# A hybrid decoder layer on one core: squares of the first norm off GpSimd, a third score buffer, value projections of N=512, and decode retention in steps

## The chip, the cores and the metric

The kernel runs on one core of a Trainium2 chip. The metric is the device time of one execution in microseconds. All inputs start in HBM and all outputs end there. Engines are called PE (TensorE; its weight loads PEld), DVE (VectorE), ACT (ScalarE), POOL (GpSimd) and SP (SyncE, here a queue that issues transfers).

## What is computed

One layer of a decoder that mixes retention and sliding-window attention, on 1024 prompt tokens and 64 decode tokens (8 sequences of 8), with a model width of 1024. The core of the reference:

```python
hn = rms_norm(x, norm_mix_gain)
q_r, k_r, v_r, g_r, q_s, k_s, v_s = jnp.split(hn @ w_in, cuts, axis=-1)   # 4 x 512, 512, 128, 128
o_r, new_ret = retention(q_r, k_r, v_r, ret_state, chunk)                 # 8 heads of 64, chunks of 128
o_r = rms_norm(o_r) * jax.nn.silu(g_r)
q_s, k_s = rms_norm(q_s, q_norm_gain), rms_norm(k_s, k_norm_gain)
o_s = swa_prompt(...) or swa_sample(...)     # window 128, 8 query heads on 2 kv heads, sinks, ALiBi
h = x + jnp.concatenate([o_r, o_s], axis=-1) @ w_out
hf = rms_norm(h, norm_ffn_gain)
return h + jnp.square(jax.nn.relu(hf @ w_up)) @ w_down, new_ret, new_k, new_v
```

One retention step on a chunk, per head:

```python
scores = einsum('ld,md->lm', q, k) * intra
o = scores @ v + (q * q_decay) @ s
s = s * s_decay + (k * k_decay).T @ v
```

The prompt starts from a zero state and has 8 chunks; each decode sequence starts from a state of its own.

## The kernel before, in words

**Numbers.** Most products are made in fp32 accuracy from three matmuls: each operand is split into a high part (rounded, made on ACT) and a low part (the rest, made on DVE or POOL), and `mm3` (L178 to L180) adds hi x hi, lo x hi and hi x lo into one PSUM tile. In the trace, L178, L179 and L180 are these three, whatever the product. Small products in retention are plain fp32 matmuls, each of which the trace shows as two.

**Tokens.** The 1088 tokens lie in chunks of 384, 384 and 320 columns and in token tiles t = 0 to 7 of 128; tile t = 8 is the decode tile, whose last 64 rows count.

**Stages.** PE's work in the trace runs in this order.
- Front (0 to 43 us): x and the first weights are loaded; `split_scaled` makes hnh (ACT, L136) and hnl (DVE, L137) of the normed input, without the row factor, which is applied to results later. `square_sum` adds the squares for that factor into rsb: chunks 0 and 1 on POOL (L144, L146), chunk 2 on ACT and DVE (L152, L153). PE runs the attention queries (psq); their squares (sqq) are read from PSUM by ACT. `inv_rms` sums over partitions and makes the factor rst (psrm).
- Key and value projection of the attention and the rest of the queries (to 120 us).
- Attention (to some 275 us): 8 blocks of 128 queries by 2 kv heads are 16 units. Each has scores (scp, L400; scaled and masked by DVE at L402 into a tile of tag "s"), a softmax (ACT, DVE, and POOL's last multiply at L366), transposes (ppp, L371) and the product with v (po, L422). Between them PE runs the retention's query, key and gate projections (psf, psg).
- Decode attention (s8, transposes pps, product po): the result is split into mhs and mls, which are stored in `ms_hi_d` and `ms_lo_d` in DRAM.
- Value projections: `value_block(t)` makes two groups of 24 matmuls 128x256 (pst), each read by one ACT instruction into half of vtr (L581). `retention_block(8)`, the decode retention, has scores rsr8, transposed keys pkr8, the product with v ror8, the product with the state pcr8 (added to ror8 through oc), and the state update pur8. Then come prompt retention blocks t = 0 to 4, each with one value tile ahead of it: scores rsr, transposed keys pkr, outputs ror, state update pur, and transposes pm of the mixed result. Their split operands lie in one tile of slot 8 (qkb), from which the store of the decode state has to be read first.
- When the value weights are dead, `proj.close()` frees their space; mixah, mixal (L781) and the raw output weights (L789) are loaded there, and the first output projection (pso) runs among retention blocks 5 to 7.
- From 420 us on, the rest of the output projection, and the MLP in Strassen-like products (psx, psy, psz, psd).

**What sets the order.** Instructions of each engine are put in order by a scheduler that simulates the program; tiles in pools are reused, and a reused tile waits for what last read it. SP issues transfers in its own order, so that a waiting one holds back those behind it.

Of the kernel before, what the change touches and what calls it, by code (L numbers as in the profile page):

```python
# [36 lines left out]
def hymba_layer(ctx: ExitStack, tc: tile.TileContext, a: dict, o: dict):  # L37
# [101 lines left out]
    def square_sum(acc, src, k, nm, pool=False):  # L139

        cw = src.shape[-1]
        if pool:
            sq = acc if k == 0 else sp.tile([P, 384], F32, tag="qkst", name=f"sq{nm}_{k}")[:, :cw]
            nc.gpsimd.tensor_tensor(sq, src, src, ALU.mult)  # L144
            if k:
                nc.gpsimd.tensor_tensor(acc, acc, sq, ALU.add)  # L146
            return
        if k == 0:
            nc.scalar.activation(acc, src, AF.Square)
        else:  # L150
# [2 lines left out]
            nc.vector.tensor_tensor(acc, acc, sq[:, :cw], ALU.add)  # L153
# [142 lines left out]
    for k in range(8):  # L296
        square_sum(rsb[:, 768:1088], xs[2][:, k, :], k, "m2")
# [81 lines left out]
    def swa_block(c):  # L379
# [5 lines left out]
        for kv in range(2):  # L385
# [8 lines left out]
            st = sp.tile([P, 4, 256], F32, tag="s", name="s" + nm)  # L394
# [70 lines left out]
    s8 = sp.tile([P, 4, 256], F32, tag="s", name="s8")[:, :, :192]  # L465
# [81 lines left out]
    w_v = [wload(a["w_in"][9 + i], 8, f"wv{i}") for i in range(2)]  # L547
# [26 lines left out]

    vts = {}

    def value_block(t):
        vt = vts[t] = rp.tile([P, 512], F32, tag="vt", name=f"vtr{t}", bufs=5)
        for i in range(2):
            ps = proj_tok(t, w_v[i], psA.tile([P, 512], F32, tag="mm", name="pst"))  # L580
            nc.scalar.activation(vt[:, i * 256 : i * 256 + 256], ps[:, :256], AF.Copy, scale=rst[:, t : t + 1])  # L581

    def retention_block(t):
        nonlocal state
        off, _, _ = tok_tile(t)
        nm = f"r{t}"
        vt = vts[t]
        qt, kt, gt = loaded8 if t == 8 else ret_load(t)

        pts = []  # L590
        if t == 8:
            for hh in range(2):
                ps = psB.tile([P, 512], F32, tag="t1", name="rs" + nm)
                p0 = hh * 64
                for p_ in range(4):
                    nc.tensor.matmul(
                        ps[64:128, p_ * 64 : p_ * 64 + 64], kt[p0 : p0 + 64, p_, 64:128], qt[p0 : p0 + 64, p_, 64:128],
                        start=True, stop=True,
                    )
                pt = rp.tile([P, 4, 128], F32, tag="rpt", name="rpt" + nm, bufs=3)  # L600
                nc.vector.tensor_tensor(
                    pt[64:128, :, 64:128], ps[64:128, :256].rearrange("p (h l) -> p h l", h=4),
                    intraS[64:128, hh::2, 64:128], ALU.mult,
                )
                pts += [pt[:, p_, :] for p_ in range(4)]
            pts = [pts[(h % 2) * 4 + h // 2] for h in range(8)]
        else:

            nc.scalar.copy(kh, kt)
            nc.gpsimd.tensor_tensor(kl, kt, kh.bitcast(F32), ALU.subtract)  # L610
            for hh in range(2):
                q_ = slice(hh * 64, hh * 64 + 64)
                nc.scalar.copy(qbh[q_, :, hh, :], qt[q_])
                nc.vector.tensor_tensor(qbl[q_, :, hh, :], qt[q_], qbh[q_, :, hh, :].bitcast(F32), ALU.subtract)
            for i in range(2):
                ps = psB.tile([P, 512], F32, tag="t1", name="rs" + nm)
                for p_ in (2 * i, 2 * i + 1):
                    cc = (p_ % 2) * 256
                    mm3(ps[:, cc : cc + 256], kh[:, p_, :], kl[:, p_, :], qbh[:, p_, :, :], qbl[:, p_, :, :], True, True)
                pt = rp.tile([P, 4, 128], F32, tag="rpt", name="rpt" + nm, bufs=3)  # L620
                nc.vector.tensor_tensor(
                    pt, ps.rearrange("p (h l) -> p h l", h=4), intra[:, 4 * i : 4 * i + 4, :], ALU.mult
                )
                pts += [pt[:, h, :] for h in range(4)]

        pk = psB.tile([P, 512], F32, tag="t2", name="pk" + nm)
        for p_ in range(4):
            nc.tensor.transpose(pk[:, p_ * 128 : p_ * 128 + 128], kt[:, p_, :], ident)
        kd = rp.tile([P, 512], F32, tag="kd", name="kd" + nm, bufs=1)
        nc.vector.tensor_tensor(  # L630
            kd.rearrange("p (h d) -> p h d", h=8), pk.rearrange("p (h d) -> p h d", h=8),
            (kdec8 if t == 8 else kdec).unsqueeze(2).broadcast_to([P, 8, 64]), ALU.mult,
        )

        cross = 0 < t < 8
        rr = slice(64, 128) if t == 8 else slice(0, 128)
        nr = 64 if t == 8 else 128
        po = psB.tile([P, 512], F32, tag="t3", bufs=1, name="ro" + nm)
        for h in range(8):
            for q_ in (slice(64, 128),) if t == 8 else (slice(0, 64), slice(64, 128)):  # L640
                nc.tensor.matmul(
                    po[q_, h * 64 : h * 64 + 64], pts[h][rr, q_], vt[rr, h * 64 : h * 64 + 64],
                    start=h == 0, stop=h == 7 and t == 0,
                )
        if t == 8:

            for hh in range(2):
                r_ = slice(hh * 64, hh * 64 + 64)
# [4 lines left out]
            pc = psB.tile([P, 512], F32, tag="t2", name="pc" + nm)
            pcv = pc.rearrange("p (q h b n) -> p q h b n", q=4, h=2, b=4)
            for p_ in range(4):
                for bp in range(4):
                    nc.tensor.matmul(
                        pcv[:, p_, :, bp, :], s0[:, p_, 2 * bp : 2 * bp + 2, :].rearrange("p b e -> p (b e)"),
# [658 lines left out]
```

## Time and profile before

| what | value |
|---|---|
| median of 3 runs | 1229.61 us (1229.16 to 1233.59) |
| profiled execution | 1229.86 us |
| its span on the core | 1228.1 us |
| busy: PE, DVE, POOL, ACT | 97%, 70%, 45%, 41% |
| chain that ended last | PE 79%, DVE 10%, DMA 4%, POOL 3% |
| mean granted PE clock | 0.986 |

The span is what the profiler saw on the engines; the profiled execution's own time has 1.8 us more around it. A row of a table by stretch has the stretch, its length, then busy time and instruction count of PE, PEld, DVE, ACT and POOL, the granted clock as a share of full speed, the busy share of the DMA engines, and GB/s. A row of the timeline has start, duration, engine, line, operation, output and inputs, shapes, how many instructions it joins, and in brackets how long the engine had been idle and for what. Matmuls are pipelined: what counts is the time from one start to the next.

### The profile page before, as it was taken

The numbers are of one execution on the slowest core, as the hardware profiler recorded it, in microseconds if no ns is written. First come the engines' busy times: TensorE is split into PE (matmuls) and PEld (weight loads), VectorE is DVE, ScalarE is ACT, GpSimd is POOL, SyncE is SP. The second block draws the span as 40 slices with busy tenths as digits, with TensorE's granted clock in tenths as the row PEclk, the third lists the DMA queues.
The fourth block names the chain that finished last, engine by engine and source line by source line (L and its number), as shares of the span: only waits on it lengthen the run. The fifth ranks groups of instructions, "written<-read, shape, count | busy, mean of one in ns | idle before, by whom it ended". The sixth has DMA issues, their size and how long they took to land.

```text
span 1228.1 us, 23929 instructions
## 1 busy us (share of the span) xinstructions
PE 1192.1 (97%) x9621; PEld 1151.4 (94%) x9621; DVE 855.1 (70%) x1508; ACT 502.2 (41%) x1032; POOL 558.1 (45%) x463
## 2 busy tenths in 40 slices
PE   7999999998998999989999999999999999999998
PEld 6999989897977899889999999999989999999998
DVE  7856776734036878788767666666578779888776
ACT  6343444572023434454444444444463333333231
POOL 8425333332225546467666666666672232253000
PEclk9999999999799999899999999999989999999999
DMA  6211234332316644433434444444584455543215
GB/s 238 71 60 60 95 99 161 100 111 72 107 53 205 211 137 132 145 104 121 167 130 146 144 143 152 143 152 160 173 299 146 142 179 166 188 166 127 74 56 182
DMA packets 102277, 169.46 MB, mean 138 GB/s; under 512 B 11999, under 2 KB 68255, under 8 KB 101911
## 3 DMA queue, kind: packets, MB, share of 16 engines
q1 hardware_dynamic: 88279, 123.24, 30.1%
q10 hardware_dynamic: 11328, 35.79, 8.9%
q0 software_dynamic: 2560, 8.91, 2.3%
q8 instruction: 75, 1.23, 0.4%
q14 instruction: 35, 0.29, 0.1%
HBM read 114.30 MB, written 53.61 MB: 137 GB/s over the span
## 4 chain that ended last, share of the span: by engine, by line
PE 79%; DVE 10%; DMA 4%; POOL 3%; issue 2%; ACT 2%; SPq 0%; ACTq 0%; DVEq 0%; POOLq 0%
PE psd L179 8%; PE psd L180 8%; PE psd L178 8%; PE psx L178 5%; PE psx L180 5%; PE psx L179 5%; PE psf L179 2%; PE psf L180 2%; PE psf L178 2%; PE psz L178 2%; PE psz L180 2%; PE psz L179 2%; PE pst L178 2%; PE pst L179 2%; PE pst L180 2%
## 5 line engine op out<-in xcount | busy, mean ns | idle before, releaser
L178 PE MATMUL psd<-uh,wd_w 128*128 128x272 f32 x896 | 259.4, 290 | 2.2 <-ACT a L1183 2.2
L179 PE MATMUL psd<-uh,wd_w 128*128 128x272 f32 x896 | 260.7, 291 | 0.6 <-DVE wd_w L758 0.6
L180 PE MATMUL psd<-ul,wd_w 128*128 128x272 f32 x896 | 259.1, 290 | 0.8 <-DVE ul L758 0.8
L178 PEld LDWEIGHTS psd<-uh,wd_w 128*128 128x128 f32 x896 | 170.4, 190 | 2.4 <-ACT a L1183 2.4
L180 PEld LDWEIGHTS psd<-ul,wd_w 128*128 128x128 f32 x896 | 169.8, 190 | 1.0 <-DVE ul L758 1.0
L179 PEld LDWEIGHTS psd<-uh,wd_w 128*128 128x128 f32 x896 | 169.7, 189 | 1.1 <-DVE wd_w L758 1.1
L1187 DVE TENSOR_TENSOR a<-a,psd 128x272 f32<-128x272 f32 x248 | 101.1, 429 | 40.8 <-PE psd L180 40.8
L758 DVE TENSOR_TENSOR wu_w<-wu_s,wu_w 128x512 fp32r<-128x512 f32 x64 | 59.5, 929 | 50.3 <-ACT wu_w L757 49.3
L757 ACT CAST wd_w<-wd_s 128x512 fp32r<-128x512 f32 x64 | 37.3, 619 | 116.8 <-PE psd L180 101.0
L758 DVE TENSOR_TENSOR ul<-ur,uh 128x1088 fp32r<-128x1088 f32 x56 | 83.1, 1510 | 2.1 <-ACT uh L757 2.1
L179 PE MATMUL psx<-op_0h,wu_w 128*128 128x272 f32 x256 | 74.2, 290 | 2.0 <-DVE wu_w L758 2.0
L178 PE MATMUL psx<-op_0h,wu_w 128*128 128x272 f32 x256 | 74.8, 292 | 0.7 <-ACT m L1066 0.5
L178 PE MATMUL psx<-op_1h,wu_w 128*128 128x272 f32 x256 | 74.7, 292 | 0.5 <-ACT m L1066 0.5
L1052 DVE SCALAR_TENSOR_TENSOR m<-m,rsf 128x272 f32<-128x272 f32 x96 | 73.2, 762 | 2.7
L180 PE MATMUL psx<-op_1l,wu_w 128*128 128x272 f32 x256 | 74.5, 291 | 0.0
L180 PE MATMUL psx<-op_0l,wu_w 128*128 128x272 f32 x256 | 74.4, 291 | 0.0
L179 PE MATMUL psx<-op_1h,wu_w 128*128 128x272 f32 x256 | 74.2, 290 | 0.0
L366 POOL TENSOR_TENSOR sp<-sp,ssp 128x1024 f32<-128x1024 f32 (+1 forms) x16 | 28.6, 1787 | 94.7 <-DVE ssp L365 69.5
L1094 POOL TENSOR_TENSOR r4t<-r3t,r4t 128x272 f32<-128x272 f32 x64 | 64.0, 1011 | 1.2
L757 ACT CAST uh<-ur 128x1088 fp32r<-128x1088 f32 x56 | 59.6, 1099 | 11.4 <-PE psd L179 9.1
L178 PE MATMUL psf<-hnh,wqk_hi 128*128 128x384 f32 (+1 forms) x192 | 63.2, 329 | 0.0
L180 PE MATMUL psf<-hnl,wqk_hi 128*128 128x384 f32 (+1 forms) x192 | 63.0, 328 | 0.0
(329 smaller groups left out, 3798.3 us busy)
## 6 DMA issues: line engine op xcount, KB each, us to landing
ur<-u_d SPq DMA_DIRECT2D x52, 544.0 KB, 5.0
u_d<-r4t SPq DMA_DIRECT2D x32, 544.0 KB, 3.9
wu_r<-in_w_up ACTq DMA_DIRECT2D x32, 512.0 KB, 4.3
wd_r<-in_w_down ACTq DMA_DIRECT2D x30, 512.0 KB, 6.9
u_d<-r3t SPq DMA_DIRECT2D x32, 408.0 KB, 3.1
y<-in_xY POOLq DMA_DIRECT2D x16, 272.0 KB, 3.2
y_d<-y POOLq DMA_DIRECT2D x16, 272.0 KB, 3.4
yt<-y_d SPq DMA_DIRECT2D x16, 272.0 KB, 3.9
```

The costliest lines, as they stand in the source:

```text
L178: nc.tensor.matmul(ps, lh, rh, start=first, stop=False, skip_group_check=more)
L179: nc.tensor.matmul(ps, ll, rh, start=False, stop=False, skip_group_check=more)
L180: return nc.tensor.matmul(ps, lh, rl, start=False, stop=last, skip_group_check=more)
L366: nc.gpsimd.tensor_tensor(s, s, ss.unsqueeze(2).broadcast_to([P, 4, n]), ALU.mult)
L757: nc.scalar.copy(hi, src)
L758: lo_eng.tensor_tensor(lo, src, hi.bitcast(F32), ALU.subtract)
L1052: nc.vector.scalar_tensor_tensor(t_, src, 0.0, rsf[:, s, h, :], ALU.max, ALU.mult)
L1094: sub = lambda o_, p_, q_: nc.gpsimd.tensor_tensor(o_, p_, q_, ALU.subtract)
L1187: nc.vector.tensor_tensor(to, to, ps, ALU.add)
```

## The change

It has five parts.
1. All squares of the first norm are made on ACT and added on DVE (`squares_of`): 16 squares and 14 adds of 128x384 leave POOL. The adds of one chunk are written behind the splits of the next.
2. The tag "s" of the attention has three buffers, where it had two.
3. The value weights are laid out in two halves of k with 512 columns each, so a token tile takes 24 matmuls 128x512 and one eviction 128x512.
4. The decode retention is a generator of seven steps, which `queued` starts behind the last matmul of a value tile, and whose last matmul the next value tile follows. From t = 1 on, value tile t + 3 is queued behind retention block t, not ahead of it.
5. Tiles are placed under others that are dead by then: dummy tiles fix the order of the pool rp and of a new pool rv (for v, mixed results, decayed queries, loaded queries and keys). The split operands of retention 0 to 4 lie in three weight tiles ("raw"), and those of 5 to 7 in slot 8.

```diff
-    def square_sum(acc, src, k, nm, pool=False):
+    def square_sum(acc, src, k, nm):
         cw = src.shape[-1]
-        if pool:
-            sq = acc if k == 0 else sp.tile([P, 384], F32, tag="qkst", name=f"sq{nm}_{k}")[:, :cw]
-            nc.gpsimd.tensor_tensor(sq, src, src, ALU.mult)
-            if k:
-                nc.gpsimd.tensor_tensor(acc, acc, sq, ALU.add)
-            return
...
     for c, (c0, cw) in enumerate(CH):
...
         hn.append((hi, lo))
+        if c:
+            squares_of(c - 1)
...
-            st = sp.tile([P, 4, 256], F32, tag="s", name="s" + nm)
+            st = sp.tile([P, 4, 256], F32, tag="s", name="s" + nm, bufs=3)
...
-    w_v = [wload(a["w_in"][9 + i], 8, f"wv{i}") for i in range(2)]
+    w_v = [wload(a["w_in"][9 + i], 4, f"wv{i}") for i in range(2)]
...
     def value_block(t):
-        vt = vts[t] = rp.tile([P, 512], F32, tag="vt", name=f"vtr{t}", bufs=5)
-        for i in range(2):
-            ps = proj_tok(t, w_v[i], psA.tile([P, 512], F32, tag="mm", name="pst"))
-            nc.scalar.activation(vt[:, i * 256 : i * 256 + 256], ps[:, :256], AF.Copy, scale=rst[:, t : t + 1])
+        vt = vts[t] = rv.tile([P, 512], F32, tag="vt", name=f"vtr{t}", bufs=5)
+        _, c, r = tok_tile(t)
+        ps = psA.tile([P, 512], F32, tag="mm", name="pst")
+        for k in range(8):
+            lh, ll = (x[:, k, r : r + 128] for x in hn[c])
+            ins = mm3(ps, lh, ll, w_v[k // 4][0][:, k % 4, :], w_v[k // 4][1][:, k % 4, :], k == 0, k == 7)
+        nc.scalar.activation(vt, ps, AF.Copy, scale=rst[:, t : t + 1])
+        return ins.ins
...
-    for t in (8, 0, 1, 2):
-        value_block(t)
-    mt8 = retention_block(8)
...
+    def queued(ins, f, *args):
+        with tc.issue_after(ins):
+            return f(*args)
+
+    decode = retention_decode()
+    value_block(8)
+    ins = value_block(0)
+    ins = queued(ins, next, decode)
+    ins = queued(ins, value_block, 1)
+    ins = queued(ins, next, decode)
+    ins = queued(ins, value_block, 2)
+    ins = queued(ins, next, decode)
...
+    qbh, qbl, kh, kl = split_space([ring.tile([P, 1024], F32R, tag="raw", name=f"qk{i}", bufs=3) for i in range(3)])
...
     for t in range(5):
-        if t < 5:
-            value_block(t + 3)
+        if t == 0:
+            for _ in range(2):
+                ins = queued(ins, next, decode)
+            ins = queued(ins, value_block, 3)
+            for _ in range(2):
+                ins = queued(ins, next, decode)
         held[t] = retention_block(t)
+        if t:
+            ins = queued(ins, value_block, t + 3)
```

Three places show how the order changes. First, DVE in the front. In both, hnl are the low parts of the normed input (L137), wq_lo and wkv_lo those of weights, rq and qs results of the queries; before:

```order
L137 SCALAR_TENSOR_TENSOR hnl_167<-x_75,c_g_mix,hnh_166 128x384 x2
L79 TENSOR_TENSOR wq_lo<-wq_raw_90,wq_hi 128x512
L137 SCALAR_TENSOR_TENSOR hnl_167<-x_75,c_g_mix,hnh_166 128x384 x2
L137 SCALAR_TENSOR_TENSOR hnl_185<-x_76,c_g_mix,hnh_184 128x384 x5
L289 COPY rq<-prq 128x6
L137 SCALAR_TENSOR_TENSOR hnl_185<-x_76,c_g_mix,hnh_184 128x384
L289 COPY rq<-prq 128x6
L137 SCALAR_TENSOR_TENSOR hnl_185<-x_76,c_g_mix,hnh_184 128x384 x2
L137 SCALAR_TENSOR_TENSOR hnl_203<-x_77,c_g_mix,hnh_202 128x320 x2
L113 TENSOR_SCALAR qg_115<-c_qkg 128x1
L111 TENSOR_SCALAR nsinks<-c_sinks 128x9
```

and after, where the adds of the squares are L147:

```order
L147 TENSOR_TENSOR rsb<-rsb,sqm_6_218 128x384
L137 SCALAR_TENSOR_TENSOR hnl_185<-x_76,c_g_mix,hnh_184 128x384 x2
L147 TENSOR_TENSOR rsb<-rsb,sqm_7_221 128x384
L137 SCALAR_TENSOR_TENSOR hnl_185<-x_76,c_g_mix,hnh_184 128x384 x2
L147 TENSOR_TENSOR rsb<-rsb,sqm_1_243 128x384
L137 SCALAR_TENSOR_TENSOR hnl_185<-x_76,c_g_mix,hnh_184 128x384
L147 TENSOR_TENSOR rsb<-rsb,sqm_2_246 128x384
L137 SCALAR_TENSOR_TENSOR hnl_185<-x_76,c_g_mix,hnh_184 128x384 x2
L113 TENSOR_SCALAR qg_115<-c_qkg 128x1
L111 TENSOR_SCALAR nsinks<-c_sinks 128x9
L137 SCALAR_TENSOR_TENSOR hnl_185<-x_76,c_g_mix,hnh_184 128x384
L147 TENSOR_TENSOR rsb<-rsb,sqm_3_249 128x384
```

The adds stand among the splits; of the 14 adds of chunks 0 and 1, ten stand ahead of the splits of chunk 2 (hnl_225, which begin right behind the last row), one among these and three behind them. The results of the queries (rq, qs), which stood among the splits of chunks 1 and 2, now come behind all of them.

Second, PE at the decode attention: pps are its transposes, po its product, pst the first value tiles, psg gate projections. Before, 72 value matmuls have gone ahead, and the two steps stand back to back:

```order
L179 MATMUL pst<-wv_hi,hnl_203 128x256
L180 MATMUL pst<-wv_lo,hnh_202 128x256
L371 MATMUL pps<-c_ident,s_2171 128x128 [waits PE_49,Pool_49]
L371 MATMUL pps<-c_ident,s_2171 128x128 [waits Activation_49] x3
L371 MATMUL pps<-c_ident,s_2171 64x128 [waits PE_49]
L371 MATMUL pps<-c_ident,s_2171 64x128 x3
L495 MATMUL po_2239<-pt_2237,v_285 64x256 [waits DVE_49]
L495 MATMUL po_2239<-pt_2237,v_285 64x256
L498 MATMUL po_2239<-pt_2230,smp 64x32 [waits DMAHW7_49]
L498 MATMUL po_2239<-pt_2230,smp 64x32 x15
L178 MATMUL pst<-wv_hi,hnh_166 128x256 [waits Activation_49]
L179 MATMUL pst<-wv_hi,hnl_167 128x256
```

After, 19 gate matmuls follow the transposes; the last three of these, and what stands behind them:

```order
L172 MATMUL psg<-hnh_224,wg_hi 128x320
L173 MATMUL psg<-hnh_224,wg_lo 128x320
L174 MATMUL psg<-hnl_225,wg_hi 128x320
L172 MATMUL pst<-wv_hi,hnh_224 128x512 [waits DVE_49]
L173 MATMUL pst<-wv_hi,hnl_225 128x512
L174 MATMUL pst<-wv_lo,hnh_224 128x512
L172 MATMUL pst<-wv_hi,hnh_224 128x512
L173 MATMUL pst<-wv_hi,hnl_225 128x512
L174 MATMUL pst<-wv_lo,hnh_224 128x512
L172 MATMUL pst<-wv_hi,hnh_224 128x512
L492 MATMUL po_2239<-pt_2237,v_285 64x256 [waits DVE_49]
L492 MATMUL po_2239<-pt_2237,v_285 64x256
```

So 19 gate and seven value matmuls stand between the transposes and the product. On ACT, the evictions of the value tiles that follow, before:

```order
L505 CAST mhs<-po_2239 128x8x4x8 [waits DMAHW6_49,PE_49]
L581 ACTIVATE vtr_3393<-pst,rst 128x256 [waits DMAHW5_49,DMAHW3_49,DVE_49]
L581 ACTIVATE vtr_3393<-pst,rst 128x256
L581 ACTIVATE vtr_3446<-pst,rst 128x256
L581 ACTIVATE vtr_3446<-pst,rst 128x256 [waits PE_49]
```

and after (qk are the split operands of retention 0, filled with zeros at L929):

```order
L502 CAST mhs<-po_2239 128x8x4x8 [waits DMAHW3_49,PE_49]
L592 ACTIVATE vtr_3413<-pst,rst 128x512 [waits PE_49,Pool_49]
L929 ACTIVATE qk_3587<-qdec 128x1024 [waits DMAHW2_49,Pool_49]
L929 ACTIVATE qk_3588<-qdec 128x1024 [waits Pool_49]
L592 ACTIVATE vtr_3440<-pst,rst 128x512 [waits PE_49]
```

The first eviction waited for two transfers and now waits for PE and POOL.

Third, PE behind the last value matmul, with the retention blocks' products by the names above; before, retention 2's outputs and retention 3's scores follow it:

```order
L179 MATMUL pst<-wv_hi,hnl_203 128x256
L180 MATMUL pst<-wv_lo,hnh_202 128x256
L641 MATMUL ror_4062<-vtr_3552,rptr_4044 64x64 [waits DVE_49]
L641 MATMUL ror_4062<-vtr_3552,rptr_4044 64x64 x7
L641 MATMUL ror_4062<-vtr_3552,rptr_4053 64x64 x8
L691 MATMUL ror_4062<-state_3381,qdr_4079 128x128 [waits Pool_49]
L691 MATMUL ror_4062<-state_3381,qdr_4079 128x128 x3
L737 MATMUL pm<-c_ident,mtr_3962 128x128 [waits PE_49]
L737 MATMUL pm<-c_ident,mtr_3962 128x128 x3
L179 MATMUL rsr_4183<-qkb 128x256 [waits Pool_49]
L180 MATMUL rsr_4183<-qkb 128x256
L178 MATMUL rsr_4183<-qkb 128x256
```

After, it is followed by retention 3's outputs and update and retention 5's scores:

```order
L173 MATMUL pst<-wv_hi,hnl_225 128x512
L174 MATMUL pst<-wv_lo,hnh_224 128x512
L721 MATMUL ror_3996<-vtr_3606,rptr_3978 64x64 [waits DVE_49,Activation_49]
L721 MATMUL ror_3996<-vtr_3606,rptr_3978 64x64 x7
L721 MATMUL ror_3996<-vtr_3606,rptr_3987 64x64 x8
L729 MATMUL ror_3996<-state_3386,qdr_4013 128x128 [waits Pool_49]
L729 MATMUL ror_3996<-state_3386,qdr_4013 128x128 x3
L736 MATMUL pur_4019<-vtr_3606,kdr_3994 64x64 [waits DVE_49]
L736 MATMUL pur_4019<-vtr_3606,kdr_3994 64x64 x7
L766 MATMUL pm<-c_ident,mtr_3916 128x128 [waits PE_49]
L766 MATMUL pm<-c_ident,mtr_3916 128x128 x3
L172 MATMUL rsr_4245<-qkb 128x256 [waits Activation_49]
```

Retention 2's outputs, and the scores of retention 3 and 4, stand ahead of the last value tile.

More of the change, by code (lines that the diff above doesn't have):

```diff
@@ L201, in hymba_layer, with squares_of @@
     rsb = nt.tile([P, T], F32, tag="rsb", name="rsb", bufs=1)
+    def squares_of(c):
+        c0, cw = CH[c]
+        for k in range(8):
+            square_sum(rsb[:, c0 : c0 + cw], xs[c][:, k, :], k, f"m{c}")
     for c, (c0, cw) in enumerate(CH):
@@ L295, in hymba_layer @@
     proj_q(0, w_q0)
-    for k in range(8):
-        square_sum(rsb[:, 768:1088], xs[2][:, k, :], k, "m2")
+    squares_of(2)
     sl8 = slot(8, F32R, "kk")
@@ L464, in hymba_layer @@
     nc.sync.dma_start(o["vc"][0:120], vc[8:128])
-    s8 = sp.tile([P, 4, 256], F32, tag="s", name="s8")[:, :, :192]
+    s8 = sp.tile([P, 4, 256], F32, tag="s", name="s8", bufs=3)[:, :, :192]
     for tt in range(2):
@@ L534, in hymba_layer @@
     rp = ret.enter_context(tc.tile_pool(name="ret", bufs=2, reuse_waits="tile"))
+    for tag, n in (("gt", 4), ("osq", 1), ("kd", 1)):
+        for i in range(n):
+            rp.tile([P, 512], F32, tag=tag, name=f"{tag}_", bufs=n)
     def ret_load(t):
@@ L537, in ret_load @@
         qt, kt = (
-            rp.tile([P, 4, 128], F32, tag=n + "8" * (t == 8), name=f"{n}{t}", bufs=1 + (t < 8)) for n in ("qt", "kt")
+            (rp if t == 8 else rv).tile([P, 4, 128], F32, tag=n + "8" * (t == 8), name=f"{n}{t}", bufs=1 + (t < 8))
+            for n in ("qt", "kt")
         )
@@ L573, in hymba_layer @@
     nc.vector.tensor_tensor(ident2, ident[:, 0:64], ident[:, 64:128], ALU.add)
+    for i in range(3):
+        rp.tile([P, 512], F32, tag="rpt", name="rpt_", bufs=3)
+    rv = ret.enter_context(tc.tile_pool(name="retv", bufs=2, reuse_waits="tile"))
+    for tag, n in (("vt", 5), ("mt", 2), ("qd", 1)):
+        for i in range(n):
+            rv.tile([P, 512], F32, tag=tag, name=f"{tag}_", bufs=n)
     vts = {}
     def value_block(t):
-        vt = vts[t] = rp.tile([P, 512], F32, tag="vt", name=f"vtr{t}", bufs=5)
@@ L579, in value_block @@
-        for i in range(2):
-            ps = proj_tok(t, w_v[i], psA.tile([P, 512], F32, tag="mm", name="pst"))
[L581 to L624, printed above, removed]
@@ new lines, in value_block, with scaled_keys @@
+        vt = vts[t] = rv.tile([P, 512], F32, tag="vt", name=f"vtr{t}", bufs=5)
+        _, c, r = tok_tile(t)
+        ps = psA.tile([P, 512], F32, tag="mm", name="pst")
+        for k in range(8):
+            lh, ll = (x[:, k, r : r + 128] for x in hn[c])
+            ins = mm3(ps, lh, ll, w_v[k // 4][0][:, k % 4, :], w_v[k // 4][1][:, k % 4, :], k == 0, k == 7)
+        nc.scalar.activation(vt, ps, AF.Copy, scale=rst[:, t : t + 1])
+        return ins.ins
+    def scaled_keys(kt, dec, nm, tag="kd"):
@@ L626, in retention_block @@
         pk = psB.tile([P, 512], F32, tag="t2", name="pk" + nm)
         for p_ in range(4):
[L628 to L629 removed]
+            ins = nc.tensor.transpose(pk[:, p_ * 128 : p_ * 128 + 128], kt[:, p_, :], ident)
+        kd = (rv if tag == "mt" else rp).tile([P, 512], F32, tag=tag, name="kd" + nm, bufs=1 + (tag == "mt"))
         nc.vector.tensor_tensor(
             kd.rearrange("p (h d) -> p h d", h=8), pk.rearrange("p (h d) -> p h d", h=8),
[L632 removed]
+            dec.unsqueeze(2).broadcast_to([P, 8, 64]), ALU.mult,
@@ L633, in retention_block @@
         )
[L635 to L644, printed above, removed]
@@ L719, in retention_block, with head_norm @@
+        return kd, ins
+    def head_norm(po, mt, rr, nm):
+        nr = rr.stop - rr.start
         sq = rp.tile([P, 512], F32, tag="osq", name="osq" + nm, bufs=1)
@@ L724, in retention_block @@
         nc.gpsimd.tensor_tensor(r[rr], r[rr], mhalf[rr].broadcast_to([nr, 8]), ALU.pow)
-        mt = mixtok8 if t == 8 else rp.tile([P, 512], F32, tag="mt", name="mt" + nm)
         nc.vector.tensor_tensor(
@@ L931, in hymba_layer @@
     mix_block(4, *held[4])
+    sl8c = slot(8, F32R, "qkb")
+    qbh, qbl, kh, kl = split_space([sl8c[:, i : i + 1024] for i in (0, 1024, 2048)])
     for t in (5, 6, 7):
```

233 lines of the change are left out of this document (149 added, 84 removed).

## Prediction

> **What bounds the kernel now.** I read the page's first part and its chain, then busy time by stretch, then PE's waits stretch by stretch, and last single lines.
>
> ```profile
> span 1228.1 us, 23929 instructions
> PE 1192.1 (97%) x9621; PEld 1151.4 (94%) x9621; DVE 855.1 (70%) x1508; ACT 502.2 (41%) x1032; POOL 558.1 (45%) x463
> ```
>
> PE (TensorE) is busy 97% of the span, so time can only come from three things: less matmul work, PE's waits, or stretches in which the granted clock is halved. The table by stretch (columns: length, busy time of PE, weight loads, DVE, ACT, POOL, then granted clock, DMA share, GB/s) says where these lie.
>
> ```profile
> 0.00:42.75 42.75, 35.31 (x252) 29.25 (x253) 35.71 (x41) 20.63 (x38) 34.31 (x45) 1.00 0.50 173
> 289.34:384.78 95.44, 89.52 (x753) 78.97 (x752) 33.44 (x59) 24.80 (x47) 32.12 (x27) 0.93 0.26 72
> 384.78:397.63 12.85, 9.76 (x135) 8.91 (x134) 9.07 (x25) 4.37 (x8) 6.15 (x6) 1.00 0.97 340
> 397.63:420.00 22.37, 19.71 (x200) 18.53 (x199) 17.38 (x34) 9.79 (x19) 11.97 (x11) 0.92 0.80 251
> 420.00:1228.10 808.10, 791.79 (x6364) 786.45 (x6363) 605.00 (x957) 326.93 (x648) 389.43 (x330) 0.99 0.45 149
> ```
>
> PE stands in the front (0 to 43 us), around the value projections (289 to 385) and around the first output projection (385 to 420). The change touches all three. From 420 us on it touches nothing but the last retention blocks, and I take that stretch as it is.
>
> **Squares off GpSimd.** In the front, PE waits for the low parts of the normed input (hnl, L137 on DVE).
>
> ```profile
>   DVE hnl L137: 13.2, 24
> L271 ACT ACTIVATE sqq<-psq x5: 437/490/493, 19.7 to 41.5; 128x384 f32<-128x384 f32 x4, 128x320 f32<-128x320 f32 x1
> L137 DVE SCALAR_TENSOR_TENSOR hnl<-x,c_g_mix,hnh 128x384 fp32r<-128x384 f32 x16 | 17.6, 1144 | 5.0 <-ACT hnh L136 5.0
> L137 DVE SCALAR_TENSOR_TENSOR hnl<-x,c_g_mix,hnh 128x320 fp32r<-128x320 f32 x8 | 9.2, 1200 | 0.0
> L79 DVE TENSOR_TENSOR wq_lo<-wq_raw,wq_hi 128x512 fp32r<-128x512 f32 x4 | 4.2, 1049 | 1.2 <-ACT wq_hi L77 1.2
> 5.09 0.62 DVE L137 SCALAR_TENSOR_TENSOR hnl<-x,c_g_mix,hnh 128x384 fp32r<-128x384 f32 x1 [4.15 <-ACT hnh L136]
> 5.70 0.69 DVE L79 TENSOR_TENSOR wq_lo<-wq_raw,wq_hi 128x512 fp32r<-128x512 f32 x1
> 49.13 0.48 DVE L153 TENSOR_TENSOR rsb<-rsb,sqm 128x320 f32<-128x320 f32 x1
> ```
>
> The first line is PE's and its weight loads' wait for hnl before the query projection (us, times). The same hnl instruction takes 0.62 us while GpSimd is idle (at 5.09) and 1.14 to 1.20 on average beside GpSimd's squares (34.31 us of GpSimd in this stretch); wq_lo takes 0.69 against 1.05. With GpSimd out of the way the 24 hnl cost 24 x 0.62 = 14.9 instead of 26.8 (-11.9) and the four wq_lo -1.4. DVE takes over 14 adds: 0.48 x 384/320 = 0.58 each, 8.1 us. That is 5.2 us off DVE; and in the new order 3 of the adds (1.7) stand behind the last hnl, so the last hnl is some 7 us earlier. ACT takes 16 squares at 0.49 (the sqq row), 7.8 us, into 22 us of idle (20.63 busy of 42.75): free. PE's five groups of 24 query matmuls, whose last result is read at 41.5, end 7 us sooner. Part comes back: the squares now end on DVE, behind the splits, so the inverse root that every eviction of the kv projection needs is hardly earlier, and PE can only fill with the rest of the queries. I take **-6**; ends 0 (that root sets the pace) and -9 (the 13.2 us of waits less what x's arrival keeps).
>
> **Third score buffer.** Between 42.75 and 298 us PE waits for two things only:
>
> ```profile
> PE po L422 <- ACT ptp L411: 0.4, 1, 0.4
> PE scp L400 <- DVE sp L402: 0.2, 1, 0.2
> 167.18 1.89 POOL L366 TENSOR_TENSOR sp<-sp,ssp 128x1024 f32<-128x1024 f32 x1 [3.23 <-ACT qxp L392]
> 169.34 0.60 PE L371 MATMUL ppp<-c_ident,sp 128*128 128x128 f32 x4
> ```
>
> So the gain is at most 0.6. The order does change: gate projections move behind the last unit, so each of the 16 attention units has about 1 us less matmul work under its softmax. In the tightest unit GpSimd's last multiply ends at 169.07 and the transposes start at 169.34, 0.27 later. Where the slack is that small the 1 us becomes a wait. I take **+1**; ends -0.6 and +8 (half a microsecond in every unit).
>
> **Around the decode attention, 298 to 310.**
>
> ```profile
> 299.03 1.09 PE L371 MATMUL pps<-c_ident,s 128*128 128x128 f32 x8 [0.77 <-POOL s L366]
> 301.06 0.65 PE L495 MATMUL po<-pt,v 64*64 64x256 f32 x4 [0.94 <-DVE pt L490]
> 306.04 0.40 PE L178 MATMUL pst<-wv_hi,hnh 128*128 128x256 f32 x1 [3.27 <-ACT vtr L581]
> 305.51 1.20 ACT L581 ACTIVATE vtr<-pst,rst 128x256 f32<-128x256 f32 x3 [2.33 <-DMA ms_hi_d<-mhs]
> 306.28:309.69 3.41, 3.41 (x18) 3.41 (x18) 0.00 (x0) 0.44 (x2) 1.45 (x2) 0.50 0.97 254
> ```
>
> Before, 72 value matmuls are used up ahead of the transposes; nothing is left to cover them, and the first eviction vtr waits for the stores of mhs and mls, under which its tile lies, with all three PSUM tiles full. In the new order 19 gate and 7 value matmuls stand between these steps, and vtr8 waits for no store. So 0.77 + 0.94 + 3.27 = 5.0 go, and so does the half clock that follows at once (3.41 at 0.50: 1.7). **-6.7**. What could be late instead is the second half of the value weights: its low part is made on GpSimd, and the order has PE wait for it twice in the first token tile. Ahead of that stand 27 wide matmuls and the decode attention, some 8 us, so I cost it at nothing; other end +3.
>
> **Decode retention in steps.**
>
> ```profile
> 326.76:337.00 10.24, 10.24 (x50) 8.23 (x49) 1.59 (x3) 0.00 (x0) 2.04 (x2) 0.50 0.01 2
> 337.00:384.78 47.78, 46.84 (x418) 39.62 (x417) 22.19 (x42) 14.87 (x25) 18.07 (x15) 1.00 0.21 62
> 323.50 2.09 PE L657 MATMUL pcr<-tabS,s0v 128*128 128x32 f32 x18
> 329.99 1.97 PE L679 MATMUL pur<-s0v,kdr 64*64 64x512 f32 x4
> 331.89 0.58 PE L178 MATMUL pst<-wv_hi,hnh 128*128 128x256 f32 x1
> ```
>
> No PE wait stands in the first stretch, but its 10.24 us run at half clock, which costs 5.1. They begin 3.3 us after the first pcr and last into the value matmuls that follow. In steps, 24 wide matmuls stand between; the longest run of small ones is 16 ror and 32 pcr (as the trace counts them), the latter 3.7 us at 2.09/18 = 0.116 each. I take **-5.1**, other end -1.7 (halves of 3.41 us, two of which stay).
>
> By the Trainium skill (TensorE: Matmul & The Clock Gate, section What's actually happening) the clock halves after an idle window of about 3.4 us. That agrees with 306.28, right behind the 3.27 us wait, but not with 326.76, where the trace shows no idle; taken strictly it would leave these 5.1 us where they are, and the sum at 1214.
>
> **N=512.**
>
> ```profile
> 311.82 0.28 PE L180 MATMUL pst<-wv_lo,hnh 128*128 128x256 f32 x1
> 311.94 0.28 PE L178 MATMUL pst<-wv_hi,hnh 128*128 128x256 f32 x1
> L178 PE MATMUL pst<-wv_hi,hnh 128*128 128x256 f32 x144 | 43.1, 300 | 3.6 <-ACT vtr L581 3.6
> 276.03 0.34 PE L180 MATMUL psg<-hnl,wg_hi 128*128 128x384 f32 x1
> 276.20 0.33 PE L178 MATMUL psg<-hnh,wg_hi 128*128 128x384 f32 x1
> ```
>
> Start to start is 0.120 us at N=256 and 0.172 at 384: 52 ns per 128 columns, so an estimated 0.224 at 512. 432 matmuls (3 x 144) become 216: 216 x (0.240 - 0.224) = **-3.5**; ends 0 and -5. The evictions halve in number (18 to 9) and double in size, on an ACT that is idle most of this stage.
>
> The Trainium skill (same page, section Back-to-back issue gap) gives about 131 ns sustained at N=512, which would save 216 x 0.109 = 23.5 instead; the 172 ns measured at 384 already exceed it.
>
> **The moved work and the loads behind the last value matmul.** Retention 3 and 4 now start ahead of the last value tile, not behind it.
>
> ```profile
> 384.76 0.52 SPq L781 DMA_DIRECT2D mixah<-ms_hi_d  x1
> 384.78 1.15 PE L641 MATMUL ror<-vtr,rptr 128*64 128x64 f32 x32
> 385.86 1.16 PE L691 MATMUL ror<-state,qdr 128*128 128x128 f32 x8
> 386.86 0.60 PE L737 MATMUL pm<-c_ident,mtr 128*128 128x128 f32 x4
> 391.12 0.69 PE L698 MATMUL pur<-vtr,kdr 128*64 128x64 f32 x16
> 397.75 0.39 PE L178 MATMUL pso<-mixah,woa 128*128 128x272 f32 x1
> ```
>
> The loads of mixah, mixal and the output weights go into space that the value weights free, so they start when the last value matmul ends (384.76), and the first output matmul comes 13.0 us later, at a DMA share of 0.97. That gap stays. Before, 9.76 us of PE work lie in it. After, retention 3's ror, pur and pm, retention 5's scores and retention 4's remainder do: two ror at 2.1 (384.78 to 386.86), two pur at 0.7 and 12 scores at 0.12 are 7.0, and 12 transposes (two pm, one pkr), whose ends overlap, an estimated 0.9: 7.9. PE idles 5.1 instead of 3.1, **+2**; the 2.7 us of waits from 397.63 to 420 should halve, since one retention block lies there instead of two, **-1**; the 0.94 us of waits between 337 and 385 (47.78 less 46.84) go, **-1**. A halved clock behind the gap is there before (0.92 of 22.37) and stays. On SP nothing is new ahead of mixah but retention 5's two loads and one gate load, whose buffers are free before the last value tile ends. The store of the decode state now holds back ACT's fill of retention 5's space alone, with a value tile's 24 matmuls (5.4 us) of cover. Ends for this part: -2 and +8, the loads being the least known.
>
> **Sum.** -6 + 1 - 6.7 - 5.1 - 3.5 + 2 - 1 - 1 = -20.3. The profiled execution took 1229.86 us, 0.25 over the median, so 1229.6 - 20.3 = **1209**.
>
> **Rivals.**
> 1. The half clock stays: the step of ror and pcr, or the longer idle ahead of the output projection, halves it again. For it: halving came 3.3 us into the pcr. Against: the wide matmuls between. It gives 1211 (one stretch of 3.41 at half clock) to 1214; I say 1213.
> 2. The front gives nothing, since the inverse root, now behind the splits on DVE, holds PE: 1215. Against it: the 13.2 us wait names hnl and nothing else.
> 3. The last loads swallow more: they are bound by DMA at 0.97, and any load held in SP's row ahead of mixah (it waits for GpSimd and DVE) moves the first output matmul one for one. With 6 to 8 us: 1216.
> 4. Slower: with 1 us less work under each softmax, PE waits at the transposes in every unit. The slack is 0.27 us in the tightest unit. To pass the old time by 0.5% this must cost 20 + 6 = 26 us, 1.6 in each of the 16 units, which is more than the 1 us taken from under it unless DVE's queue also slips: 1236 or more.
> 5. The change does not do what it says: squares on ACT and DVE cost what GpSimd's did, and the steps wait for each other. Then only the 6.7 and 3.5 are left, and the moved loads eat part: 1223.
>
> **How the numbers follow.** The forecast has 0.55, rivals 1 to 3 have 0.14, 0.10 and 0.10, rival 4 has 0.05 and rival 5 0.06. The forecast's own range is 1202 to 1217. Leaving out rivals 4 and 5 and the ends of the rest, the range is 1199 to 1221. 0.5% is 6.1 us, about what a measurement of this kernel can tell from no change: faster means under 1223.5. All of the forecast and rivals 1 to 3 lie there, less 0.04 for their tails, and half of rival 5: 0.88. Within 0.5%: 0.07. Slower: 0.05.
>
> **What would show it.** hnl near 0.62 us and the fifth sqq near 34 us; no vtr waiting for a store; clock 1.00 between the decode attention and the last value matmul; pst at about 0.224 us start to start; last value matmul near 369 and first pso 13 us later. The prediction is wrong if PE's waits for hnl give way to waits for rst, if transposes in the attention wait for GpSimd, or if the first pso comes later than 13 us after the last pst.

## Result and the profile after

The changed kernel took 1211.25 us (median of 4 runs, 1209.06 to 1213.15) against 1231.3 for the kernel before beside it (1229.16 to 1233.59): a ratio of 0.9836, 95% interval 0.9807 to 0.9865. The forecast was 1209 with a range of 1199 to 1221. A repeat beside 11 runs of the kernel before gave 1211.18 and 0.9852 (0.9837 to 0.9868). The profiled execution took 1210.2 us. One execution of the kernel with the third buffer, the squares and N=512 (below) took 2647.8 us and is left out of its times.

Its page and its table by stretch, with the columns used above:

```profile
span 1208.4 us, 23493 instructions
PE 1176.6 (97%) x9405; PEld 1128.5 (93%) x9405; DVE 847.7 (70%) x1522; ACT 504.5 (42%) x1039; POOL 522.8 (43%) x433
```

```profile
0.00:42.75 42.75, 37.25 (x300) 33.58 (x300) 28.58 (x62) 28.53 (x57) 0.83 (x15) 1.00 0.57 196
...
286.00:369.90 83.90, 83.90 (x598) 65.93 (x596) 36.48 (x68) 26.56 (x40) 38.15 (x30) 1.00 0.32 91
369.90:383.73 13.83, 10.14 (x137) 9.27 (x137) 9.44 (x27) 3.85 (x7) 5.25 (x6) 0.88 0.94 341
383.73:505.00 121.27, 116.80 (x1055) 114.00 (x1054) 101.08 (x181) 52.59 (x109) 66.43 (x71) 0.99 0.51 160
```

In the front PE issues 300 matmuls in 42.75 us, not 252. From the first value matmul (286) to the last (369.9) it never stands, and the clock is full; before, 95.44 us held 5.9 us of waits and a clock of 0.93. The gap ahead of the output projection is still there: 13.8 us with 10.14 busy.

Lines of the front, the decode attention, the value tiles and that gap; the first is PE's and its weight loads' wait for hnl:

```profile
  DVE hnl L137: 3.0, 9
L137 DVE SCALAR_TENSOR_TENSOR hnl<-x,c_g_mix,hnh 128x384 fp32r<-128x384 f32 x16 | 9.3, 610 | 4.5 <-ACT hnh L136 4.5
282.38 1.04 PE L368 MATMUL pps<-c_ident,s 128*128 128x128 f32 x8
286.27 0.40 PE L173 MATMUL pst<-wv_hi,hnl 128*128 128x512 f32 x1
286.51 0.39 PE L174 MATMUL pst<-wv_lo,hnh 128*128 128x512 f32 x1
369.67 0.39 PE L174 MATMUL pst<-wv_lo,hnh 128*128 128x512 f32 x1
369.87 0.52 SPq L810 DMA_DIRECT2D mixah<-ms_hi_d  x1
383.73 0.37 PE L172 MATMUL pso<-mixah,woa 128*128 128x272 f32 x1
```

hnl takes 0.610 us instead of 1.144. The wait for it, 3.0 here and 13.2 before, adds up PE and its weight loads, which stand at the same time: PE alone stood 0.6 us for hnl, before 4.6. The decode attention's transposes come at 282.38 with no wait named, not at 299.03. Value matmuls of N=512 have a median of 0.227 us from start to start. The loads still start with the last value matmul, and the first output matmul is 13.9 us behind them.

### The profile page after: what moved, and what is told of

Its sections match the earlier page's. It is cut to its first block, busy times and chain, and to the rows that moved or that the text cites. A ratio compares the mean times of both kernels' runs of the same rounds, so it can differ in the third digit from the quotient of the medians.

```text
span 1208.4 us, 23493 instructions
## 1 busy us (share of the span) xinstructions
PE 1176.6 (97%) x9405; PEld 1128.5 (93%) x9405; DVE 847.7 (70%) x1522; ACT 504.5 (42%) x1039; POOL 522.8 (43%) x433
## 4 chain that ended last, share of the span: by engine, by line
PE 77%; DVE 10%; DMA 6%; issue 3%; POOL 2%; ACT 1%; SPq 0%; ACTq 0%; DVEq 0%; POOLq 0%
PE psd L173 8%; PE psd L174 7%; PE psd L172 7%; PE psx L172 5%; PE psx L174 5%; PE psx L173 5%; PE psz L172 2%; PE psz L174 2%; PE psz L173 2%; PE pst L172 2%; PE pst L173 2%; PE pst L174 2%; PE psf L172 2%; PE psf L174 2%; PE psf L173 2%
## 5 line engine op out<-in xcount | busy, mean ns | idle before, releaser
L787 DVE TENSOR_TENSOR wu_w<-wu_s,wu_w 128x512 fp32r<-128x512 f32 x64 | 63.5, 993 | 50.1 <-ACT wu_w L786 49.0
```

Of the source, the lines that this page charges most:

```text
L787: lo_eng.tensor_tensor(lo, src, hi.bitcast(F32), ALU.subtract)
```

## Experiments

Each was timed beside the kernel before; times are medians, ratios are to the kernel before with their 95% intervals. Four are built on the kernel before and add parts to it, the others take parts from the changed kernel or move them. Of each edit the lines that matter are shown.

**Squares back on GpSimd.**

```diff
-            square_sum(rsb[:, c0 : c0 + cw], xs[c][:, k, :], k, f"m{c}")
+            square_sum(rsb[:, c0 : c0 + cw], xs[c][:, k, :], k, f"m{c}", c < 2)   # True: on GpSimd
```

> The changed kernel with the first norm's squares of chunks 0 and 1 back on GpSimd. Theory (GpSimd's squares slow DVE's low parts): hnl back at 1.1 to 1.2 us each, PE's waits in the front back by some 6 us, time 1211 + 4 to 6 = 1215 to 1217. Rival (the front is bound by the arrival of x and the splits on ACT, and the gain came from elsewhere): hnl still slow, but time within 1 us of 1211.

The edit also puts the calls back to where they stood before. 1217.02 us, 0.9898 (0.9883 to 0.9913): 5.8 more than the changed kernel. PE's wait for hnl and its duration, from the trace of this run:

```profile
  DVE hnl L137: 12.8, 22
L137 DVE SCALAR_TENSOR_TENSOR hnl<-x,c_g_mix,hnh 128x384 fp32r<-128x384 f32 x16 | 18.0, 1167 | 4.0 <-ACT hnh L136 4.0
```

The theory held: the duration nearly doubles when GpSimd works beside it, and the time follows.

**Two score buffers.**

```diff
-            st = sp.tile([P, 4, 256], F32, tag="s", name="s" + nm, bufs=3)
+            st = sp.tile([P, 4, 256], F32, tag="s", name="s" + nm)
```

> The changed kernel with two score buffers in the attention, as before. Theory (PE waited 0.2 us for a score buffer before, so a third one gives nothing): 1211 within 1 us, PE's waits in the attention unchanged. Rival (with about 1 us less matmul work under each unit the third buffer is needed): waits at the scores, up to 8 us, 1212 to 1219.

The tile of the decode attention's scores (s8) has the same edit. 1229.69 us, 1.0005 (0.9993 to 1.0017). Both theories fell: without the third buffer nothing is left of the change. The wait is not at the scores of a unit. PE's timeline around the decode attention, waits alone:

```profile
303.65 1.97 PE L368 MATMUL pps<-c_ident,s 128*128 128x128 f32 x8 [7.66 <-POOL s L363]
306.40 1.12 PE L492 MATMUL po<-pt,v 64*64 64x256 f32 x4 [0.77 <-DVE pt L487]
315.69 1.57 PE L628 MATMUL rsr<-qt,kt 64*64 64x64 f32 x16 [6.33 <-DMA kt<-kr_d]
```

The scores of the attention's last unit (scp) and those of the decode attention (sc); the first two lines are the changed kernel, the last two this run:

```profile
243.23 0.28 PE L398 MATMUL scp<-kl,qxp 128*128 128x256 f32 x1
271.83 0.29 PE L473 MATMUL sc<-k,q 64*32 64x64 f32 x8
268.18 0.28 PE L398 MATMUL scp<-kl,qxp 128*128 128x256 f32 x1
295.71 0.29 PE L473 MATMUL sc<-k,q 64*32 64x64 f32 x8
```

With two buffers the last unit's scores come 25 us later in PE's order, and the last score matmul of the decode attention, which follows that unit's product, at 295.8 instead of 271.9. No long wait names the score tile (the longest, for DVE's sp, is 0.6 us): the buffer acts through the order that the scheduler chooses. By then the gate projections are used up (the last at 279.6; with three buffers 285.9, 14 us behind the scores). PE stands 7.7 us for the softmax, 6.3 us for the loads issued behind the stores, and runs at half clock between.

**N=256 in the changed kernel.**

```diff
-        ps = psA.tile([P, 512], F32, tag="mm", name="pst")
...
+        for i in range(2):
+            n_ = slice(i * 256, i * 256 + 256)
+            ps = psA.tile([P, 512], F32, tag="mm", name="pst")[:, :256]
...
+            nc.scalar.activation(vt[:, n_], ps, AF.Copy, scale=rst[:, t : t + 1])
```

> The changed kernel with each value tile as two groups of 24 matmuls of N=256 and two evictions, weights laid out as in the changed kernel. Theory (only the start to start time matters: 0.227 us at 512 against 0.120 at 256): +216 x 0.013 = 2.8 us, 1214. Rival (the value tiles only fill time in which retention's chains run): 1211 to 1212.

1211.78 us, 0.9855 (0.9838 to 0.9872), against 0.9852 for the repeat of the changed kernel. The expected 2.8 us (0.23%) are not seen, though the intervals are too wide to exclude them. What N=512 saves in matmuls is at most a small part of the gain.

**Decode retention in one block, in the changed kernel.** Value tiles 1 and 2 go ahead, and the seven steps follow each other.

```diff
-    ins = queued(ins, next, decode)
     ins = queued(ins, value_block, 1)
-    ins = queued(ins, next, decode)
     ins = queued(ins, value_block, 2)
-    ins = queued(ins, next, decode)
+    for _ in range(3):
+        ins = queued(ins, next, decode)
```

> The changed kernel with value tiles 1 and 2 ahead of the decode retention and its seven steps without value tiles between them, value tile 3 behind. Theory (a long run of small matmuls halves the clock): a stretch of 3.4 to 10.2 us at clock 0.50 within the decode steps or right behind them, +1.7 to +5.1 us and some waits between the steps, 1213 to 1217. Rival (the halved clock before came from the wait at 306 us and what followed it, not from the small matmuls): clock 1.00 throughout, 1211 to 1212.

1222.73 us, 0.9932 (0.991 to 0.9954): 11.5 more by the median, but the six runs spread from 1215.4 to 1223.41, so the loss is 4 to 12. The profile is of an execution of 1222.46 us. The table by stretch of this run, and two of PE's waits:

```profile
315.50:319.00 3.50, 3.50 (x23) 3.32 (x23) 1.99 (x4) 0.62 (x1) 0.00 (x0) 0.59 0.00 0
322.40:325.80 3.40, 2.55 (x11) 0.99 (x10) 2.66 (x5) 1.23 (x2) 3.40 (x4) 1.00 0.23 67
329.00:332.60 3.60, 3.60 (x10) 0.99 (x10) 1.45 (x3) 0.60 (x1) 1.04 (x1) 0.50 0.00 0
...
381.60:396.00 14.40, 5.50 (x79) 5.06 (x77) 8.33 (x18) 3.75 (x6) 6.33 (x6) 0.79 0.99 346
```

```profile
PE pso L172 <- ACT woa L786: 8.9, 1, 8.9
PE pur L683 <- POOL s0v L678: 1.5, 1, 1.5
```

The clock halves from 314.9 to 318.3, with PE busy throughout since 309, and again from 328.7 to 338.8: 13.7 us in all, which cost 6.8, more than the 5.1 expected. The rest is order: the state update has no value matmuls left between its steps and waits for GpSimd, and the gap ahead of the output projection has 5.5 us of work in it instead of 10.1, so that PE waits 8.9 us for the loads.

**The changed kernel again.**

> The changed kernel once more, beside the others of this call. All theories: 1211 within 2 us; its profile says how far the last stage (the second product of the MLP, 356.6 us in the first profile against 351.5 before), which the change does not touch, repeats: within 2 us of 356.6 if the earlier start itself makes it longer, anywhere from 351 to 357 if it is chance.

1211.18 us. In this run the clock does halve among the decode steps:

```profile
309.80:313.20 3.40, 3.40 (x10) 2.68 (x9) 0.69 (x2) 0.00 (x0) 0.00 (x0) 0.52 0.00 0
```

This is the same program as in the first profile, where no such stretch lies between 286 and 369.9. So the steps don't end the halving. In these profiles it was shorter and less certain with them: over the six with steps in their order and three score buffers it took 0 to 7 us, over the six with a decode block 7 to 14. The last stage repeats at 356.2 us (849.2 to 1205.4).

**The third buffer alone, on the kernel before.** The edit is the two-buffer one the other way.

> The kernel before with the third score buffer alone. Theory (the third buffer lets the decode attention's scores go ahead, so that gate and value projections cover its waits): the waits of 0.8, 0.9 and 3.3 us and the half clock after them go, 6.7 us, while the half clock of the decode retention in one block stays: 1222 to 1225. Rival (the third buffer pays only with the decode steps): 1229 within 1 us.

1220.3 us, 0.9925 (0.9911 to 0.9939): 9.3 less, where at most 7.6 were expected. The transposes, which waited 0.77 us at 299.03, come at

```profile
282.11 1.03 PE L371 MATMUL pps<-c_ident,s 128*128 128x128 f32 x8
```

and the waits of 0.94 and 3.27 are gone with them, while the decode block's half clock stays (321.9 to 332). By the last value matmul 4.6 us are gained (384.6 to 380.0). Another 4.6 come in the output projection (131.0 to 126.4 us), where the clock is 0.99 instead of 0.96, and 1.1 are lost in the gap between; why the clock holds better there is not shown.

**The squares alone, on the kernel before.**

```diff
         hn.append((hi, lo))
+        if c:
+            p0, pw = CH[c - 1]
+            for k in range(8):
+                square_sum(rsb[:, p0 : p0 + pw], xs[c - 1][:, k, :], k, f"m{c - 1}")
```

> The kernel before with the first norm's squares off GpSimd alone. Theory (5 to 6 us of PE's waits in the front go, independent of the rest): 1223 to 1225. Rival (the lead is absorbed at the next bound, since the decode attention waits there): 1227 to 1229.

The calls on GpSimd are gone. 1234.76 us, 1.0044 (1.0029 to 1.0059): slower. The front's gain is there, the gate projections end 9.8 us earlier, and all of it is lost at one place:

```profile
301.49 1.97 PE L372 MATMUL pps<-c_ident,s 128*128 128x128 f32 x8 [7.66 <-POOL s L367]
304.24 1.12 PE L496 MATMUL po<-pt,v 64*64 64x256 f32 x4 [0.78 <-DVE pt L491]
311.21 0.58 PE L178 MATMUL pst<-wv_hi,hnh 128*128 128x256 f32 x1 [4.00 <-ACT vtr L582]
```

Half clock lies around these waits from 298 to 315, where the kernel before had 3.4 us of it. With the scores of the decode attention as late as two buffers put them, work done sooner on PE is cover that is missing later. The rival had the mechanism, not the sign.

**Third buffer and squares, on the kernel before.**

> The kernel before with the third score buffer and the squares off GpSimd, nothing else. Theory (with two buffers the attention's chain, not PE, sets the end of the decode attention, so that a faster front was lost there; with three PE sets it): the front's 5 to 6 us come through, 1220.3 - 5.8 = 1214 to 1215. Rival (the squares on ACT and DVE disturb the attention whatever its buffers): 1220 or more.

1213.29 us, 0.9868 (0.9853 to 0.9884). The squares, worth +5.2 with two buffers, are worth -7.0 with three. These two parts give 16 of the 18 us.

**These two and N=512, on the kernel before,** with neither steps nor tiles under dead ones.

```diff
-        for i in range(2):
-            ps = proj_tok(t, w_v[i], psA.tile([P, 512], F32, tag="mm", name="pst"))
+        ps = psA.tile([P, 512], F32, tag="mm", name="pst")
+        for k in range(8):
+            lh, ll = (x[:, k, r : r + 128] for x in hn[c])
+            mm3(ps, lh, ll, w_v[k // 4][0][:, k % 4, :], w_v[k // 4][1][:, k % 4, :], k == 0, k == 7)
```

> The kernel before with the third score buffer, the squares off GpSimd and the value projections of N=512; no steps, no tiles under dead ones. In its order all value tiles are done ahead of prompt retention 0, and the output loads follow there. Theory (the first two parts carry the gain; N=512 is worth 216 x 0.013 = 2.8 us of matmul time wherever it stands, and steps and tiles bring nothing beyond it): 1213.3 - 2.8 = 1210.5, within 2 us of the changed kernel. Rival (the steps are needed: the decode retention in one block keeps its half clock of 7 to 10 us, 3.5 to 5 us of time, and what N=512 saves is lost among retention's chains): 1213 to 1216. A third way: with the loads started earlier and retention 1 to 4 as their cover, the gap ahead of the output projection closes: 1207.

1223.58 us, 0.996 (0.9942 to 0.9978): by the ratios some 11 more than with N=256, beyond all three expectations. The scheduler now runs all value tiles ahead of the outputs of prompt retention 0 (last value matmul at 357.9, outputs at 358.2), and retention is left without cover:

```profile
371.00:402.00 31.00, 23.74 (x253) 20.78 (x252) 27.36 (x59) 13.69 (x24) 15.97 (x11) 0.87 0.65 210
```

```profile
PE rsr L178 <- ACT qkb L613: 4.4, 3, 2.2
PE pur L702 <- DVE kdr L634: 1.6, 2, 1.3
PE ror L645 <- DVE mtr L730: 0.5, 1, 0.5
```

In these 31 us PE stands 7.3, of which 6.5 are the three waits shown, and the clock averages 0.87. I read from this what the queued order does for the changed kernel: it keeps a value tile between retention blocks. No run takes the queue alone out of the changed kernel.

**Value tiles ahead of the retention blocks, in the changed kernel.**

```diff
-        held[t] = retention_block(t)
         if t:
             ins = queued(ins, value_block, t + 3)
+        held[t] = retention_block(t)
```

> The changed kernel with value tile t + 3 queued ahead of retention block t, not behind it, for t = 1 to 4. Theory (the loads behind the last value matmul take 14 us whatever runs then; ending the value tiles earlier starts them earlier and leaves retention 3 and 4 as cover): last value matmul 5 us earlier, first output matmul 5 us earlier, PE's idle time ahead of it 3.7 us less and no half clock: 1206 to 1208. Rival (retention then lacks matmuls to cover its own chains, so the waits only move): 1210 to 1213.

1215.32 us, 0.9881 (0.9864 to 0.9897): 4 more. The last value matmul came at 371.6, not 5 us earlier, and the first output matmul waited:

```profile
386.99 0.56 PE L172 MATMUL pso<-mixah,woa 128*128 128x272 f32 x1 [5.61 <-DMA mixah<-ms_hi_d]
```

The loads of mixah went behind those of the weights on SP (375.1 instead of 369.9 us), and the clock halved for 7 us at 310. Both expectations were missed, since neither had foreseen the order on SP.

**Output loads in halves, in the changed kernel.** The first raw output weights are loaded ahead of mixah, and the second half's output matmuls are queued behind the first's.

```diff
-        for x, d_ in zip("hl", (ms_hi_d, ms_lo_d)):
-            t_ = mix[s, "a" + x] = pl.tile([P, 4, 2, Q], F32R, tag="mixa" + x, name=f"mixa{x}{s}")
...
+        for h in range(2):
+            for x, d_ in zip("hl", (ms_hi_d, ms_lo_d)):
+                c_ = 2 * Q * s + Q * h
+                nc.sync.dma_start(mix[s, "a" + x].bitcast(F32)[:, :, h, :], d_[:, :, c_ : c_ + Q])
...
+    gens["a"], gens["r"] = (wo_pair(0, 0, x) for x in "ar")
+    ahead.append(next(gens["a"]))
     mix_load(0, mx0)
+    ahead.append(next(gens["r"]))
```

> The changed kernel with the first raw output weights loaded ahead of mixah and mixal, these loaded in halves of 272 columns, and the second half's output matmuls queued behind the first's. Theory (behind the last value matmul PE stands because what the first output matmul needs comes in 2.7 MB, and retention's chains alone don't fill the gap): the first output matmul 5 to 8 us behind the last value matmul instead of 14, PE's idle time ahead of it 1 us or less instead of 3.7, fewer half clocks: 1206 to 1209. Rival (PE waits there for retention's chains on DVE and GpSimd, not for the loads, and output matmuls only move the wait): 1210 to 1212.

1210.27 us, 0.9837 (0.9816 to 0.9858): not to be told from the changed kernel. The first output matmul came 6.6 us earlier, and the wait moved to retention's chain (PE's ror waited 2.6 us for DVE's mtr), with the clock halved from 383.9 to 390.7. The rival held: with the wait for the loads gone, the time is the same.

**The step of ror and pcr cut in two, in the changed kernel,** value tile 2 between the halves and value tile 3 ahead of the state update.

```diff
-            if p_ == 3:
+            if p_ % 2:
                 yield ins.ins
```

> The changed kernel with the decode step of ror and pcr cut in two, a value tile between the halves and value tile 3 ahead of the state update. Theory (the clock halves when small matmuls run for some 4 us or more, as they did in the repeated profile at 309.8 us and not in the first): clock 1.00 throughout the decode retention; time 1209 to 1212, since the update's own waits lose a value tile as cover. Rival (the halving is independent of the small matmuls' run): a half clock near 305 to 315 us as in the repeat.

1215.97 us, 0.9887 (0.9872 to 0.9902). The time missed the theory's 1209 to 1212. There is no half clock near 310, as the theory had it, but 10.2 us of it further on, where the update and retention 0 now run without a value tile:

```profile
286.00:327.20 41.20, 40.99 (x261) 31.99 (x259) 9.49 (x15) 11.76 (x18) 16.05 (x14) 1.00 0.38 101
327.20:338.00 10.80, 9.74 (x48) 5.13 (x48) 5.14 (x9) 1.83 (x3) 5.82 (x5) 0.53 0.10 26
```

## Why the prediction was right, and where it was not

The sum was -20.3; between the two medians of the first comparison lie 20.05. The total came out, but not term by term, and in part by luck: by the end of the output projection the profiles lie 23.8 us apart (528.7 to 504.9), more than the whole sum, and behind it, where I had forecast nothing, some 4 were lost.

- **Squares, -6.** In the profile the first matmul of the next stage (psf) moved from 87.87 to 82.02, -5.9, and taking the part back cost 5.8. Size and mechanism right. The last hnl starts 11 us earlier (38.3 to 27.1), not 7. My other end of -9 was taken from the 13.2 us of waits, which count PE's 4.6 and its weight loads' 8.5 together; PE stood 7.4 us in all in this stage (42.75 less 35.31). That the gain stands by itself was wrong: alone it was +5.2. My mark for it, the fifth sqq near 34 us, failed too (40 us): part of the queries went behind the key projection.
- **Third score buffer, +1, "the gain is at most 0.6".** This is the step that failed. I bounded the buffer by the wait for a score inside the attention and called the rest a matter of order. The order hung on the buffer. Alone it gave 9.3 us, with the squares 21.5 (1234.76 to 1213.29), and without it the change gave nothing (18.5 us of loss). The chance that this was the part that decided had no rival of its own.
- **Around the decode attention, -6.7.** All three waits and the half clock behind them went. I put it down to the order around value tiles; the third buffer alone removes the waits of 0.77, 0.94 and 3.27.
- **Steps, -5.1.** In the first profile the clock is 1.00 there; in the repeat 3.4 us at 0.52 stay (1.7 us of time). The other end of my range was nearer in that run. What the steps and the queue are worth is not only the clock, and it depends on what stands beside them: with the decode block put back 4 to 12 us go, with 8.9 of PE's waits for the loads; N=512 without them costs some 11, with 7.3 of waits. Yet with N=256 and neither steps, queue nor moved tiles (third buffer and squares) only 2 us are missing.
- **N=512, -3.5.** 0.227 us from start to start, against an estimated 0.224, makes 216 x 0.013 = 2.8. In the total it does not show (1211.78 against 1211.18), and without steps and queue it cost some 11.
- **Moved work and loads, +2 - 1 - 1.** The last value matmul came at 369.67 (forecast 369), the first output matmul 13.9 us after the loads began (13.0) and 14.1 behind the last value matmul, which I had named as a sign of being wrong. PE had 10.14 us of work there, not 7.9, in part at half clock (0.88 on average), and stood 3.7 us, not 5.1, all of it for retention's chain (2.05 for kdr, 1.64 for mtr), so that the loads set this gap was wrong, as the halves showed. From there to the end of the output projection another 9.8 us were gained (131.05 to 121.27), where I had some 5: 2.3 of it waits, the rest busy time, with 1055 matmuls instead of 1125 and a clock of 0.99 instead of 0.96.
- **Not in the sum.** The last stage (the MLP's second product), which I took as it is, was 5.1 us longer in the profile; from the end of the output projection on it is some 4, since the stage between was 1 shorter.

```profile
872.30:1223.90 351.60, 347.99 (x2737) 347.10 (x2737) 276.59 (x436) 127.78 (x203) 102.08 (x68) 0.99 0.48 159
847.60:1204.30 356.70, 348.69 (x2738) 346.30 (x2736) 275.63 (x436) 127.55 (x203) 101.21 (x68) 1.00 0.48 157
```

The first line is the kernel before, the second the changed one: busy time is alike, waits are 8.0 instead of 3.6. Over the other kernels of this study the same stage took from 351.2 (third buffer and squares) to 356 us, and the changed kernel's repeat again 356.2. An earlier start alone does not set it: two kernels that entered it at the same time (third buffer and squares at 854.8, ror and pcr cut in two at 854.6) took 351.2 and 356.0. What sets it stays open.

Rival 1 was partly true: the clock halves again in the repeat and ahead of the output projection, and its 1211 to 1214 holds the measured time too, so that the total alone does not tell it from the forecast. Rivals 2, 3 and 5 did not occur. The slower rival had the place wrong: the attention's units never made PE wait for more than 0.3 us.

## What to carry to other kernels

A buffer is not bounded by the waits at its own tile: ask which work it allows to go ahead, and what that leaves as cover for the next chain. Parts of a change are not added up from their own stages when they share such cover: here one part was worth +5.2 without another and -7.0 with it. Saving matmul time paid nothing here where matmuls are the cover of another engine's chain; there, try to keep wide work between the short steps by an order of your own.

## What the runs showed of the hardware

- The clock halves without PE standing: in the kernel before 10.24 us at 0.50 with PE busy for all of it, and behind a run of small decode matmuls it showed in every profile of this study but the first of the changed kernel. By the Trainium skill (TensorE: Matmul & The Clock Gate, section What's actually happening) the clock falls to half after an idle window; here PE was busy in the records for the whole stretch, so the traces do not agree with idle time as the cause. The section also says that the window runs free of the program. That fits: the same program had the halving in one profile and not in the other.
- The half clock came in lengths of about 3.4 us and its multiples: 3.4 with the squares put back, 6.8 with the output loads in halves, 10.24 in the kernel before and with the third buffer alone.
- A DVE instruction with two SBUF operands took 1.14 to 1.17 us on average beside GpSimd's elementwise work and 0.61 alone, as the rows of hnl show (kernel before 1.14, squares put back 1.17; changed kernel 0.61).
